# Reordered start of a two-layer attention, recurrence and mixture-of-experts kernel: inputs ahead of modulation weights, constants on another queue, a later softplus, idle matmuls

## Chip, cores and metric

The kernel runs on one core of one Trainium2 chip. The metric is the device time of one execution in microseconds (us), taken as the median of a few runs. One profiled execution, with its trace, is at hand as well. Engines are named as the profile names them: PE is the matrix engine, PEld its weight loads, DVE the vector engine, ACT the scalar engine, POOL the general engine, SP the engine that here issues nearly all transfers. A q behind a name (SPq, ACTq) is the engine's sequencer, which issues and waits.

## What is computed

Layer 0 modulates a normalised x and a normalised context with vectors that come out of the conditioning by a matrix product (`ada_w`), projects both, and runs attention over a neighbourhood and a gated linear recurrence side by side. Layer 1 mixes by a Fourier transform. Each layer ends with a mixture of 16 experts. The parts that the change touches:

```python
mod = silu_c @ ada_w[layer] + ada_b[layer]
shift1, scale1, gate1, shift2, scale2, gate2 = jnp.split(mod[:, None, :], 6, axis=-1)
h = modulate(rmsnorm(x, norm_mix[layer]), shift1, scale1)
...
h_ctx = modulate(rmsnorm(ctx, norm_mix[layer]), mod_ctx[:D], mod_ctx[D:])
...
log_a = -LRU_C * r * jax.nn.softplus(-lam.astype(jnp.float32))
return jnp.exp(log_a), jnp.sqrt(-jnp.expm1(2.0 * log_a)) * (i * xc)
```

x is 256 x 1024, the context 256 x 1024, everything in 32-bit floats.

## The kernel before

All weights pass through 16 slots of 1 MB. SP issues their transfers in the order of the program, and a slot's next transfer waits until the slot is given back. The order of instructions on each engine is set by a scheduler when the program is built; an engine then runs its list strictly in that order.

The first stage works in five units of one or two of the eight 128-channel blocks (`units0`). For a unit, `load_ada` (L268) brings the needed columns of four `ada_w` tiles in four pieces, `load_wx` (L272) brings rows of the first projection's weights. `ada_te` multiplies them with the conditioning on PE (L333, tile `gv`), ACT copies the result (L339, `gvr`), PE turns it into columns (L340), and DVE adds the bias (L350, `modc`, `modx`). Meanwhile `rms_scale` normalises x into `xn` and the context in place (`xc`): ACT squares and sums (L436) and takes the root (L438), DVE inverts and scales (L439, L440). PE transposes (L501, `tp`), ACT and DVE modulate (L513, L514, L516, giving the high part and the low part of h), `split_w` splits the weights into high and low parts (L394 on ACT, L395 on POOL or DVE, `wp`), and `channels` multiplies (L407 to L409, `xb`).

The next stage multiplies h with the key weights (`kp`), while DVE runs the convolution (L597, L600, `xcT`), further `ada_w` tiles in `ada_ve` (L375, L381, `gva`) and ACT the recurrence's gates: `Recurrence.gates` gives R and I by a sigmoid (L664), `Recurrence.scan` gives A by an exponential (L672, scale `spm8`) and a tanh (L673, scale `sp4`), then DVE `lt` (L679), ACT a root (L681), DVE L684 and further. `spm8` and `sp4` come from `softplus()` (L469 to L485), some 26 small DVE operations on 128x8 values in a row, which start from `softplus_exp()` (L462, L463 on ACT). The products `kp` are copied out by ACT and DVE (L619, L617, `kq`), and the query product (`qp`) takes over their PSUM banks.

A sigmoid, exponential, root or silu on ACT needs its table; where the table changes, the trace shows an ACT_TABLE_LOAD.

Of the kernel before, what the change touches and what calls it, by code (L numbers as in the profile page):

```python
# [12 lines left out]
AF = mybir.ActivationFunctionType  # L13
# [133 lines left out]
def hybrid_layers(  # L147
# [21 lines left out]
    nc = tc.nc  # L169
    ve, ac, te, gp = nc.vector, nc.scalar, nc.tensor, nc.gpsimd  # L170
# [8 lines left out]
    def acc(name="acc"):  # L179
        return ps.tile([128, 512], F32, tag="acc", name=name)  # L180
# [16 lines left out]
    def t2k(name):  # L197
        return buf(name, "t2k", 520, 4)
# [41 lines left out]
    smA = data.tile([94, 128], F32, tag="t1k", name="smA", bufs=2)  # L240
    smB = data.tile([96, 128], F32, tag="t1k", name="smB", bufs=2)
    cst = const.tile([128, 352], F32, name="cst")
    rw = const.tile([128, 8, 32], F32, name="rw")
    rb = const.tile([128, NE], F32, name="rb")
    nc.sync.dma_start(out=smA, in_=small[0:94, :])
    nc.sync.dma_start(out=smB, in_=small[94:190, :])
    nc.sync.dma_start(out=cst, in_=consts)
    ident = cst[:, 0:128]
    ones = cst[:, 128:256]
    iota1 = cst[:, 256:320]  # L250
# [11 lines left out]
    units0 = [(0,), (1,), (2, 3), (4, 5), (6, 7)]  # L262

    def load_ada(ks):
        c = slice(ks[0] % 4 * 128, ks[-1] % 4 * 128 + 128)
        for j in (ks[0] // 4, 2 + ks[0] // 4):
            for i in range(2):
                nc.sync.dma_start(out=a_s[j].part(i)[:, :, c], in_=a_s[j].src[i][:, :, c])  # L268
# [2 lines left out]
        i, k = divmod(k, 4)  # L271
        nc.sync.dma_start(out=Wx.part(i)[:, k:k + 2], in_=Wx.src[i][:, k:k + 2])  # L272

    load_ada(units0[0])
    for tb in range(2):
        nc.sync.dma_start(out=xt[:, tb], in_=x_in[tb * 128:(tb + 1) * 128, :])
    for tb in range(2):
        nc.sync.dma_start(out=xc[:, tb], in_=ctx_in[tb * 128:(tb + 1) * 128, :])
    load_wx(0)
# [20 lines left out]
    qn = cols[:, 92:93]  # L300
    kn = cols[:, 93:94]
    ada_b = [cols[:, 94:142], cols[:, 142:190]]

    sc32 = const.tile([128, 8, 32], F32, name="sc32")
    gp.memset(sc32, 0.0)
# [91 lines left out]
    def split_w(W, eng=gp):  # L397

        t = t4k("wp").bitcast(F32R)
        h, lo = t[:, 0:512], t[:, 512:1024]  # L400
        with tc.high_priority(PRI):
            split(h, W, lo, eng)
        return h, lo

    def mm3(p, lhs, rhs, start, stop):

        te.matmul(out=p, lhsT=lhs[0], rhs=rhs[0], start=start, stop=False)  # L407
        te.matmul(out=p, lhsT=lhs[0], rhs=rhs[1], start=False, stop=False)
        te.matmul(out=p, lhsT=lhs[1], rhs=rhs[0], start=False, stop=stop)  # L409

    def scale_col(name, mod, o, gain, s=slice(0, 8)):

        if name not in a_col:
            a_col[name] = const.tile([128, 8], F32, name=name)
        ve.scalar_tensor_tensor(a_col[name][:, s], mod[:, o + s.start:o + s.stop], 1.0, gain[:, s],
                                op0=ALU.add, op1=ALU.mult)
        return a_col[name]
# [43 lines left out]
    def softplus_exp():  # L461
        ac.activation(z, lam, AF.Abs)  # L462
        ac.activation(z, z, AF.Exp, scale=-1.0)  # L463
# [25 lines left out]
    hH = [h4[k // 4][:, k % 4] for k in range(8)]  # L489
# [7 lines left out]
    def transposed(k):  # L497
        p = wps("tp")
        for i in range(4):
            src = xn if i < 2 else xc  # L500
            te.transpose(p[:, i * 128:(i + 1) * 128], src[:, i % 2, k * 128:(k + 1) * 128], ident)  # L501
        return p

    def modulate(ps_):
        ks = sorted(ps_)
        s = slice(ks[0], ks[-1] + 1)
        a = scale_col("a1", modc[0], 8, g_mix[0], s)
        b = scale_col("a1x", modx, 8, g_mix[0], s)
        h = {}
        for k in ks:  # L510
            h[k] = t2k("hm")[:, 0:512]
            for c, m, sh in ((slice(0, 256), a, modc[0]), (slice(256, 512), b, modx)):
                ac.activation(hH[k][:, c], ps_[k][:, c], AF.Identity, scale=m[:, k:k + 1], bias=sh[:, k:k + 1])  # L513
                ve.tensor_scalar(h[k][:, c], ps_[k][:, c], m[:, k:k + 1], sh[:, k:k + 1], op0=ALU.mult, op1=ALU.add)  # L514
        for k in ks:
            ve.tensor_tensor(hL[k], h[k], hH[k].bitcast(F32), op=ALU.subtract)  # L516
# [7 lines left out]
    def channels(p, w, n, k):  # L524


        for b in range(4):
            c = slice(b * 128, (b + 1) * 128)
            first, last = (True, True) if n == 512 else (b % 2 == 0, b % 2 == 1)
            mm3(p[b], (w[0][:, c], w[1][:, c]), (hH[k][:, 0:n], hL[k][:, 0:n]), k == 0 and first, k == 7 and last)  # L530
# [4 lines left out]
    def ada_first(ks):  # L535
        ada_te(0, [(a_s[j], k % 4 * 128, 4 * j + k % 4) for j in (ks[0] // 4, 2 + ks[0] // 4) for k in ks], True)()

    wx = {}
    for u in range(len(units0) + 1):
        if u < len(units0):  # L540
            ks = units0[u]
            ada_first(ks)
            tp = {k: transposed(k) for k in ks}
            modulate(tp)
            for k in ks:
                wx[k] = split_w(Wx[:, k])
        if u == 1:
            softplus_exp()
        if u:
            for k in units0[u - 1]:  # L550
                channels(xp, wx.pop(k), 512, k)

    s_bg = [a_s[0].keep(i) for i in range(2)]
    s_kq = [a_s[2].keep(i) for i in range(2)]
# [322 lines left out]
    def normed(p4, gate, into=None):  # L877

        xn = t8k("xn").rearrange("p (t c) -> p t c", t=2) if into is None else into
        table(AF.Sqrt, p4[0][:, 0:1])  # L880
        for tb in range(2):
            for h in range(2):
                add_gated(p4[tb * 2 + h], gate, tb, slice(h * 512, (h + 1) * 512))
            last = rms_scale(xt, xn, tb)
        return xn, last
# [304 lines left out]
    xn, _ = normed(mp, gate)  # L1190
# [25 lines left out]
    for gp2 in range(2):  # L1216
# [5 lines left out]
        for b in range(2):  # L1222
            k = dict(start=(b == 0), stop=(b == 1))
# [21 lines left out]
    xn, _ = normed(mp, gate)  # L1245
# [81 lines left out]
```

## Time and profile before

| quantity | value |
|---|---|
| median of 3 runs | 803.24 us (802.31 to 805.01) |
| profiled execution, own time | 804.33 us |
| its span, first to last instruction | 802.5 us |
| PE busy | 712.6 us (89%) |
| DVE busy | 353.2 us (44%) |
| ACT busy | 236.9 us (30%) |
| POOL busy | 125.2 us (16%) |
| moved by DMA | 277.33 MB, mean 346 GB/s |

Busy shares are averages over stages with different limits. What the first stage is worth has to be read in its own stretch, and followed to the first place where another wait ends later.

### The profile page before, as it was taken

The numbers are of one execution on the slowest core, as the hardware profiler recorded it, in microseconds if no ns is written. First come the engines' busy times: TensorE is split into PE (matmuls) and PEld (weight loads), VectorE is DVE, ScalarE is ACT, GpSimd is POOL, SyncE is SP. The second block draws the span as 40 slices with busy tenths as digits, with TensorE's granted clock in tenths as the row PEclk, the third lists the DMA queues.
The fourth block names the chain that finished last, engine by engine and source line by source line (L and its number), as shares of the span: only waits on it lengthen the run. The fifth ranks groups of instructions, "written<-read, shape, count | busy, mean of one in ns | idle before, by whom it ended". The sixth has DMA issues, their size and how long they took to land. (4 is left out here: it accounts for less than half of the span.)

```text
span 802.5 us, 10368 instructions
## 1 busy us (share of the span) xinstructions
PE 712.6 (89%) x4080; PEld 388.7 (48%) x4080; DVE 353.2 (44%) x648; ACT 236.9 (30%) x420; POOL 125.2 (16%) x100
## 2 busy tenths in 40 slices
PE   3999869897998899799999996978699799999986
PEld 2676557674657534244344333656434344334333
DVE  3559798898875511111121105794421121112015
ACT  6246738554555310110111003434210110011000
POOL 1132561444111201000000001051201000000002
PEclk9999988897999899999999999999799999999999
DMA  8987467563887799999999999999199999999991
GB/s 278 360 331 294 169 262 263 212 261 125 342 325 287 291 354 421 418 414 422 419 423 420 420 421 421 421 409 367 60 423 421 401 423 421 421 423 419 422 376 63
DMA packets 53789, 277.33 MB, mean 346 GB/s; under 512 B 4898, under 2 KB 20832, under 8 KB 22496
## 3 DMA queue, kind: packets, MB, share of 16 engines
q1 hardware_dynamic: 53584, 276.47, 86.3%
q8 instruction: 36, 0.59, 0.3%
q14 instruction: 25, 0.20, 0.1%
q10 hardware_dynamic: 144, 0.07, 0.0%
HBM read 275.47 MB, written 1.05 MB: 345 GB/s over the span
## 5 line engine op out<-in xcount | busy, mean ns | idle before, releaser
L1054 PE MATMUL g<-slot,xg 128*64 128x512 f32 x512 | 116.2, 608 | 8.0 <-PEq L1142 8.0
L1091 PE MATMUL dn<-slot,aT 128*64 128x512 f32 (+1 forms) x544 | 115.7, 577 | 4.1 <-DVE aT L1075 4.1
L1054 PE MATMUL u<-slot,xg 128*64 128x512 f32 x512 | 113.7, 593 | 0.8 <-DMA slot<-in_moe_u_dram 0.8
L1060 DVE TENSOR_TENSOR act<-act,u 128x512 f32<-128x512 f32 x16 | 11.0, 687 | 191.2 <-PE u L1054 191.2
L395 POOL TENSOR_TENSOR wp<-slot,wp 128x512 fp32r<-128x512 f32 x41 | 60.3, 1480 | 155.9 <-ACT wp L394 145.9
L1054 PEld LDWEIGHTS g<-slot,xg 128*64 128x64 f32 x512 | 38.3, 140 | 82.0 <-issue 81.1
L1054 PEld LDWEIGHTS u<-slot,xg 128*64 128x64 f32 x512 | 38.8, 137 | 72.9 <-issue 70.9
L381 DVE SCALAR_TENSOR_TENSOR gva<-slot,sc,gva 128x512 f32<-128x512 f32 x77 | 72.6, 943 | 1.1
L1091 PEld LDWEIGHTS dn<-slot,aT 128*64 128x64 f32 x544 | 37.9, 138 | 70.6 <-issue 61.0
L1094 DVE SCALAR_TENSOR_TENSOR yL<-dn,gcol,yH 128x512 fp32r<-128x512 f32 (+1 forms) x34 | 24.5, 720 | 99.0 <-ACT yH L1093 90.8
L1093 ACT ACTIVATE yH<-dn,gcol 128x512 fp32r<-128x512 f32 (+1 forms) x34 | 22.5, 662 | 139.9 <-PE dn L1091 139.9
L1009 ACT ACTIVATE xg<-xg,modc,a 128x256 f32<-128x256 f32 x32 | 18.0, 564 | 136.4 <-PE xg L1000 136.4
L394 ACT ACTIVATE wp<-slot 128x512 fp32r<-128x512 f32 x72 | 43.8, 625 | 46.3 <-PE mix L409 15.8
L1011 POOL TENSOR_TENSOR SG<-S,gates 128x512 f32<-128x512 f32 x8 | 8.4, 1044 | 310.4 <-PE st L1063 302.0
L1059 ACT ACTIVATE act<-g 128x512 f32<-128x512 f32 x16 | 9.6, 597 | 121.0 <-PE g L1054 121.0
L333 PE MATMUL gv<-slot,sc 128*32 128x128 f32 x832 | 34.6, 297 | 6.5 <-DVE modc L350 3.7
L333 PEld LDWEIGHTS gv<-slot,sc 128*32 128x32 f32 x832 | 27.6, 119 | 13.3 <-DVE modc L350 3.9
L1000 PE MATMUL xg<-S,xh 128*128 128x256 f32 x128 | 28.4, 306 | 3.8 <-DVE S L988 2.6
L1007 DVE TENSOR_SCALAR xg<-xg,a,modc 128x256 f32<-128x256 f32 x32 | 17.4, 543 | 29.2 <-ACT xg L1009 29.2
L395 DVE TENSOR_TENSOR wp<-slot,wp 128x512 fp32r<-128x512 f32 x31 | 25.5, 826 | 8.0 <-ACT wp L394 7.3
L1000 PE MATMUL xg<-S,xl 128*128 128x256 f32 x128 | 27.4, 298 | 0.0
L1031 PE MATMUL ya<-yH,ST 128*128 128x512 f32 x60 | 26.4, 440 | 0.6 <-ACT yH L1093 0.2
(258 smaller groups left out, 1125.5 us busy)
## 6 DMA issues: line engine op xcount, KB each, us to landing
slot<-in_moe_g_dram SPq DMA_DIRECT2D x64, 1024.0 KB, 14.2
slot<-in_moe_u_dram SPq DMA_DIRECT2D x64, 1024.0 KB, 14.4
slot<-in_moe_d_dram SPq DMA_DIRECT2D x60, 1024.0 KB, 16.5
slot<-in_ada_w_dram SPq DMA_DIRECT2D x40, 1024.0 KB, 7.4
slot<-in_w_in_dram SPq DMA_DIRECT2D x8, 1024.0 KB, 8.3
slot<-in_ada_w_dram SPq DMA_DIRECT2D x12, 512.0 KB, 9.2
slot<-in_w_out_dram SPq DMA_DIRECT2D x4, 1024.0 KB, 4.9
slot<-in_fnet_w_dram SPq DMA_DIRECT2D x4, 1024.0 KB, 19.8
```

The costliest lines, as they stand in the source:

```text
L333: te.matmul(out=p[32 * q:32 * q + 32, 0:128], lhsT=sc32[:, k, :], rhs=W[:, k, c:c + 128], start=(k == 0), stop=(k == 7))
L381: ve.scalar_tensor_tensor(r, W[:, k], sc32[:, k, 0:1], r, op0=ALU.mult, op1=ALU.add)
L394: ac.activation(dst_h, src, AF.Copy)
L395: eng.tensor_tensor(dst_l, src, dst_h.bitcast(F32), op=ALU.subtract)
L1000: at_xg[0] = te.matmul(out=p[:, i * 256:(i + 1) * 256], lhsT=xx[:, tb, k * 128:(k + 1) * 128], rhs=S[:, tb * 256:(tb + 1) * 256], start=(n ...
L1007: ve.tensor_scalar(xg[:, k], pv, a2[:, k:k + 1], b2[:, k:k + 1], op0=ALU.mult, op1=ALU.add)
L1009: ac.activation(xg[:, k], pv, AF.Identity, scale=a2[:, k:k + 1], bias=b2[:, k:k + 1])
L1031: te.matmul(out=yacc[tb * 2 + h], lhsT=ST[:, tb * 128:(tb + 1) * 128], rhs=y[:, h * 512:(h + 1) * 512], start=(p == 0 and n == 0), stop=(n ...
L1054: te.matmul(out=q[half(i), :], lhsT=xg[:, k, half(i0 + i)], rhs=W[i][:, k], start=(k == 0), stop=(k == 7))
L1091: te.matmul(out=dn[half(i), :], lhsT=aT[:, fc * 128 + 64 * i:fc * 128 + 64 * i + 64], rhs=W[i][:, fc, c], start=(fc == 0), stop=(fc == 3))
L1093: ac.activation(yH[:, c], dn, AF.Copy, scale=gcol)
L1094: ve.scalar_tensor_tensor(yL[:, c], dn, gcol, yH[:, c].bitcast(F32), op0=ALU.mult, op1=ALU.subtract)
```

## The change

Four edits. The three small loads (`smA`, `smB`, `cst`) are issued by ACT in place of SP. The two loads of x are issued ahead of the first unit's four pieces of `ada_w`. Six matmuls on constants, into a PSUM tile that nobody reads, stand ahead of the first product with `ada_w`. `softplus_exp()` is tied behind the last modulating instruction of the first stage.

```diff
-    nc.sync.dma_start(out=smA, in_=small[0:94, :])
-    nc.sync.dma_start(out=smB, in_=small[94:190, :])
-    nc.sync.dma_start(out=cst, in_=consts)
+    nc.scalar.dma_start(out=smA, in_=small[0:94, :])
+    nc.scalar.dma_start(out=smB, in_=small[94:190, :])
+    nc.scalar.dma_start(out=cst, in_=consts)
...
-    load_ada(units0[0])
     for tb in range(2):
         nc.sync.dma_start(out=xt[:, tb], in_=x_in[tb * 128:(tb + 1) * 128, :])
+    load_ada(units0[0])
...
+    warm = acc("warm")
+    for _ in range(6):
+        te.matmul(out=warm[:, 0:352], lhsT=ones, rhs=cst, start=True, stop=True)
...
+    last_h = [None]
...
-                ac.activation(hH[k][:, c], ps_[k][:, c], AF.Identity, scale=m[:, k:k + 1], bias=sh[:, k:k + 1])
+                last_h[0] = ac.activation(hH[k][:, c], ps_[k][:, c], AF.Identity, scale=m[:, k:k + 1], bias=sh[:, k:k + 1])
...
-        if u == 1:
-            softplus_exp()
...
+    with tc.issue_after(last_h[0].ins):
+        softplus_exp()
```

The scheduler answers with another order on several engines; lines behind the edits have other numbers in the changed kernel (L436 becomes L441, L664 becomes L671, L672 becomes L679).

First place: ACT from the program's start. Before:

```order
L314 DMA before<-in_tri_dram 128x128
L306 ACT_TABLE_LOAD
L306 ACTIVATE sc_127<-cols 128x8x2
L462 ACTIVATE sp_145<-cols 128x8
L324 ACT_TABLE_LOAD
L324 ACTIVATE junk<-sc_127,eps 128x1
L463 ACT_TABLE_LOAD
L463 ACTIVATE sp_145<-sp_145 128x8
L436 ACTIVATE jk,ss<-xt 128x1024 x2
L438 ACT_TABLE_LOAD
L438 ACTIVATE rs<-ss,eps 128x1 x2
L436 ACTIVATE jk,ss<-xc 128x1024 x2
```

The same place in the changed kernel, from behind the three new issues on:

```order
L441 ACT_TABLE_LOAD
L441 ACTIVATE jk,ss<-xt 128x1024
L311 ACT_TABLE_LOAD
L311 ACTIVATE sc_134<-cols 128x8x2
L319 DMA before<-in_tri_dram 128x128
L329 ACT_TABLE_LOAD
L329 ACTIVATE junk<-sc_134,eps 128x1
L443 ACTIVATE rs<-ss,eps 128x1
L441 ACTIVATE jk,ss<-xt 128x1024
L344 ACTIVATE gvr<-gv 64x128
L443 ACTIVATE rs<-ss,eps 128x1
L441 ACTIVATE jk,ss<-xc 128x1024
```

The squares of x moved ahead of and around silu, one table load went, and the copy `gvr` of the first unit's product now stands ahead of the context's squares.

Second place: DVE in the key stage, where the tail of softplus now stands (`sp` are its small tiles; L485 to L490 are the old L480 to L485, L386 is `ada_ve`, L400 the split of a weight piece). In the changed kernel:

```order
L386 SCALAR_TENSOR_TENSOR gva<-slot_589,sc_134,gva 128x512
L485 TENSOR_TENSOR sp_762<-sp_762,sp_760 128x8
L486 TENSOR_SCALAR sp_762<-sp_762 128x8
L485 TENSOR_TENSOR sp_762<-sp_762,sp_760 128x8
L486 TENSOR_SCALAR sp_762<-sp_762 128x8
L487 TENSOR_TENSOR sp_762<-sp_762,sp_758 128x8
L488 SCALAR_TENSOR_TENSOR sp_762<-sp_762,sp_150 128x8
L489 TENSOR_SCALAR spm_154<-sp_762 128x8
L490 TENSOR_SCALAR sp4c<-sp_762 128x8
L400 TENSOR_TENSOR wp<-slot_595,wp 128x512
L394 TENSOR_TENSOR modc_147<-gv,cols 128x4
```

Before, softplus stood on DVE in the first stage, 22 of its operations ahead of the first L439 and the last four between the scalings of x. Now eight of its operations stand ahead of the convolution, eight more between `ada_ve` operations, and the last ten in a row just ahead of the first split of the query weights.

Third place: ACT in the key stage. Before:

```order
L664 ACT_TABLE_LOAD
L664 ACTIVATE R<-gp,cols 128x512
L672 ACT_TABLE_LOAD
L672 ACTIVATE A<-R,spm_147 128x512
L664 ACT_TABLE_LOAD
L664 ACTIVATE R<-gp,cols 128x512 x2
L394 ACTIVATE wp<-slot_120 128x512
L664 ACTIVATE R<-gp,cols 128x512
L673 ACTIVATE R<-R,sp4c 128x512
L394 ACTIVATE wp<-slot_588 128x512
L672 ACT_TABLE_LOAD
```

The same place in the changed kernel:

```order
L671 ACT_TABLE_LOAD
L671 ACTIVATE R<-gp,cols 128x512
L399 ACTIVATE wp<-slot_120 128x512
L671 ACTIVATE R<-gp,cols 128x512 x3
L679 ACT_TABLE_LOAD
L679 ACTIVATE A<-R,spm_154 128x512
L671 ACT_TABLE_LOAD
L671 ACTIVATE I<-gp,cols 128x512
L399 ACTIVATE wp<-slot_595 128x512
L671 ACTIVATE I<-gp,cols 128x512 x2
L680 ACTIVATE R<-R,sp4c 128x512
```

The first A (which reads `spm`) moved behind all four R. The four I, the first split of the query weights and the first tanh stand behind it. Over the whole program ACT has 22 table loads where it had 26. In the expert stages nothing moved.

## Rows read from the trace of the kernel before

**Rows 1.** The page's first line.

```profile
span 802.5 us, 10368 instructions
```

**Rows 2.** Busy time by stretch: stretch, its us, engines, granted clock, DMA share, GB/s.

```profile
30.00:35.00 5.00, 5.00 (x78) 3.91 (x78) 2.49 (x8) 1.32 (x3) 1.25 (x2) 1.00 1.08 364
```

**Rows 3.** Timeline of the first 27 us: start, us, engine, line, operation, idle before it.

```profile
0.74 0.37 SPq L245 DMA_DIRECT2D smA<-in_small_dram  x1
...
2.01 2.67 SPq L268 DMA_DIRECT2D slot<-in_ada_w_dram  x4
...
8.28 3.81 PE L333 MATMUL gv<-slot,sc 128*32 128x128 f32 x30 [0.79 <-DMA slot<-in_ada_w_dram]
...
10.18 1.46 PEld L333 LDWEIGHTS gv<-slot,sc 128*32 128x32 f32 x14 [0.44 <-DMA slot<-in_ada_w_dram]
...
11.39 1.06 ACT L436 ACTIVATE jk<-xt 128x1024 bf16<-128x1024 f32 x1 [1.37 <-DMA xt<-in_x_in_dram]
...
12.67 1.06 ACT L436 ACTIVATE jk<-xt 128x1024 bf16<-128x1024 f32 x1
...
20.21 1.57 DVE L440 TENSOR_SCALAR xc<-xc,rs 128x1024 f32<-128x1024 f32 x1
...
22.35 0.56 ACT L513 ACTIVATE h<-tp,modc,a 128x256 fp32r<-128x256 f32 x1 [3.09 <-PE tp L501]
22.67 3.63 PE L333 MATMUL gv<-slot,sc 128*32 128x128 f32 x32
...
26.23 1.13 PE L407 MATMUL xb<-h,wp 128*128 128x512 f32 x2
```

**Rows 4.** One piece for the fourth unit: its issue, its landing; the unit's first product.

```profile
L268 SPq DMA_DIRECT2D slot<-in_ada_w_dram x1: 1461/1461/1461, 23.7 to 23.7; - x1
...
DMA to landing us min/median/max: 9.7/9.7/9.7
...
35.87 0.41 PE L333 MATMUL gv<-slot,sc 128*32 128x128 f32 x4
```

**Rows 5.** Timeline, DVE: the first and last of 18 alternating softplus operations.

```profile
10.91 0.17 DVE L480 TENSOR_TENSOR sp<-sp,sp 128x8 f32<-128x8 f32 x1
...
14.37 0.17 DVE L481 TENSOR_SCALAR sp<-sp 128x8 f32<-128x8 f32 x1
```

**Rows 6.** Timeline from the first to the second stage: ACT, DVE and PE.

```profile
59.05 0.63 ACT L394 ACTIVATE wp<-slot 128x512 fp32r<-128x512 f32 x1 [2.76 <-PE xb L409]
...
74.14 0.72 ACT L672 ACTIVATE A<-R,spm 128x512 f32<-128x512 f32 x1
...
80.55 1.28 ACT L672 ACT_TABLE_LOAD   x1
...
81.00 0.68 DVE L395 TENSOR_TENSOR wp<-slot,wp 128x512 fp32r<-128x512 f32 x1
...
86.41 0.16 DVE L389 TENSOR_TENSOR modc<-gv,cols 128x4 f32<-128x4 f32 x1 [4.74 <-PE gv L386]
...
87.48 5.08 DVE L381 SCALAR_TENSOR_TENSOR gva<-slot,sc,gva 128x512 f32<-128x512 f32 x3
...
96.42 0.69 DVE L617 COPY kq<-kp 128x512 f32<-128x512 f32 x1
...
97.16 0.51 PE L407 MATMUL qp<-wp,h 128*128 128x512 f32 x1 [3.29 <-DVE kq L617]
...
98.17 0.63 ACT L394 ACTIVATE wp<-slot 128x512 fp32r<-128x512 f32 x1 [3.33 <-PE qp L409]
...
100.78 1.09 DVE L684 SCALAR_TENSOR_TENSOR A<-A,R 128x512 f32<-128x512 f32 x1 [0.61 <-ACT R L681]
```

**Rows 7.** Timeline, second direction of the recurrence: ACT and DVE.

```profile
157.14 0.63 ACT L394 ACTIVATE wp<-slot 128x512 fp32r<-128x512 f32 x1 [6.97 <-PE vp L409]
...
158.42 1.28 DVE L679 SCALAR_TENSOR_TENSOR lt<-A,R 128x512 f32<-128x512 f32 x1 [2.12 <-ACT R L673]
```

**Rows 8.** Busy time by stretch, as in the second group, after two waits of PE.

```profile
110.00:120.00 10.00, 4.17 (x17) 3.58 (x17) 10.00 (x11) 1.43 (x3) 6.07 (x5) 0.79 0.56 227
```

## The prediction

> **What bounds the kernel now.** I read the share of each stretch first, then the timeline of the first 27 us, then the waits from the key product on. The span is 802.5 us of a profiled execution of 804.33 us, so 1.8 us lie outside it [rows 1]. From 22.67 us PE works without a gap worth naming [rows 2, 3], and it stays so for some 70 us. Ahead of that it waits. The reader should follow one chain: x lands at 11.39 us and its second half lets ACT go on at 12.67, ACT then squares and takes roots of x and of the context, DVE scales the context's second half at 20.21 (1.57 us), the four transposes follow, and the first modulated block starts on ACT at 22.35 us [rows 3]. Only then come 32 products for the second unit (3.63 us), and the first projection product stands at 26.23. The product for the first unit with `ada_w` was long ready: its last 14 records could start at 10.18, when the last piece landed, and ended at 8.28 + 3.81 = 12.1 us [rows 3]. So x is late and `ada_w` is early, and the DMA engines are full from then on (share 1.08 [rows 2]): what one gains the other gives.
>
> From the key product on, another chain decides: the key product's banks are copied out by DVE at 96.42, PE waits 3.29 us for that, ACT then waits 3.33 us for PE, and DVE goes on with the recurrence at 100.78 [rows 6].
>
> **Part 1, the head: x first, constants from ACT.** SP loses three issues, which held it from 0.74 until the first piece at 2.01: the large transfers start 1.27 us sooner [rows 3]. The set of constants, four pieces and x was in at 12.67 (the square started as soon as it could). With 1.27 us won, the same set is in at about 11.4, with the pieces now last. Bounds for the last piece: 10.18 (as now) and 12.67 (it simply takes x's place). I take 11.4.
>
> Then, in the new order on ACT: the second half of the product takes 1.9 us (10.18 to 12.1 [rows 3]), to 13.3; the copy and root 0.5, to 13.8; the context's first square with its read 1.25 (11.39 to 12.67 is one square and the start of the next, 1.28 [rows 3]), a root 0.2, the second square 1.25, a root 0.2: 16.7; DVE scales, between half of 1.57 and 1.57 us, and PE transposes 0.5: about 18.4. Against 22.35 that is 4.0 us. With the bounds of the last piece it is 5.2 and 2.7. Softplus leaving DVE gives nothing here, since DVE had been waiting for ACT's roots.
>
> Does the gain last to the key product? The second unit's products and everything behind them come 4.0 earlier, and the pieces of later units must be there. For the fourth unit the last piece lands at 23.7 + 9.7 = 33.4, the one that its first product needs about 1.5 us before (estimate: the issue of the last took 1461 ns, the queue being full), and the product starts at 35.87 [rows 4]. That leaves 4.0, and 1.27 more by the earlier stream: enough, but a gain over 5 would end there. So: -4.0.
>
> A rule of the skill speaks against this edit, and I weigh it here. The Trainium skill, DMA: Bandwidth & Descriptors, section "Issuing engines are not separate DMA queues", says that transfers issued from several engines run on the same 16 DMA engines, so that only issue time is saved. The trace bears on it by the share of 1.08 [rows 2]: a full set of engines has nothing to give. The sum above uses the 1.27 us of issue alone; what an exchange without that would give is a rival below.
>
> **Part 2, the idle matmuls.** Six calls of 352 columns are twelve records. Two records of 512 columns took 1.13 us at 26.23 [rows 3], so twelve of 352 take at most 12 x 0.565 x 352/512 = 4.7 us. They start when the constants are in, and PE now waits until 8.28 for a piece [rows 3], which will land later than now. Cost 0, covered by that wait; were the constants in so late that they end at 10, up to 1 us. On the good side: 32 records of 128 columns in 3.63 us at 22.67 are 113 ns each, which is the lower of the clock's two levels (128 columns at 1.2 GHz are 107 ns). Were the last half of the first unit's product at the higher level, it would take 0.95 us less. PE waits for pieces in between, so I count 0 of it, and keep -0.95 as a bound.
>
> **Part 3, softplus moved.** ACT's exponential and its table load (1.28 us [rows 6]) fall into a wait of 2.76 us for PE at 59.05 [rows 6]: no cost. The 26 DVE operations are the matter. Alternating in a row they step by (14.37 - 10.91)/17 = 0.204 us [rows 5]. Eight stand ahead of the convolution (1.6 us, of which 1.1 fall into DVE's wait for the same ACT piece), eight are spread between longer operations and cost some 0.3. The last ten stand in front of the split at 81.00 [rows 6]: ten by 0.204 is 2.0. All times here are on the old trace's clock; the head's gain shifts them together. From 81.0, less 0.6 for the `lt` that no longer stands there, plus 0.8, plus 2.0, `spm8` is there at about 83.1. DVE itself loses nothing, since it now waits 4.74 us until 86.41 [rows 6].
>
> But ACT used `spm8` at 74.14 [rows 6]. In the new order its first A waits for 83.1, and behind it, in strict order: load 1.28, A 0.72, load 1.28, one I 0.7, the first split of the query weights 0.63, two I 1.3, tanh 0.7: 89.7. Less, in the bargain, are two of six table loads up to here. DVE's `lt` needs that tanh, and now stands ahead of the `ada_ve` run that begins at 87.48 [rows 6]. So DVE is 2.2 us late, and its copy of the key product comes at 98.6 in place of 96.42. PE's wait grows from 3.29 to 5.5, ACT's split at 98.17 comes at 100.4. Between that split and the first root there stand now one more tanh and one more split, 0.7 + 0.6: DVE's L684 comes at 100.78 + 2.2 + 1.3 = 104.3, 3.5 late. Of that 0.2 to 0.6 lie in its present wait of 0.61 [rows 6]; I take 3.3. Bounds: 1.2, if DVE's run gets shorter by being later (the three operations at 87.48 take 1.7 us each, the four behind them, until 96.42, only 1.0 each, so 2.1 could be had); 5.5, if PE runs at the lower level after its longer wait (below). From there DVE has no slack for 20 us, so it stays: +3.3.
>
> On the price of a table load page and trace differ: the Trainium skill, ScalarE: Activation LUTs, section "What ACT_TABLE_LOAD costs", gives about 2.66 us for every switch, load and drain together. The row shows 1.28 and the next operation right behind [rows 6]; by the page's figure the wait above would be 2.8 us longer for its two loads (an estimate), and the measurement decides.
>
> **Part 4, further down.** In the recurrence's second direction two more loads go. ACT's split at 157.14, which waited 6.97 us for PE, still stands ahead of the second tanh, and DVE's 2.12 us wait at 158.42 with it [rows 7]. 0; bounds -1.5 and +1.
>
> **Sum.** -4.0 + 0 + 3.3 + 0 = -0.7: 803.6 for the profiled execution's own 804.33. That execution is 1.09 above the median of 803.24, so the median goes to about 802.5.
>
> **Rivals.** *The loss fades*: the head's 4.0 reaches the end, since DVE's lateness is taken up by waits it has anyway (4.74 at 86.41, 2.12 at 158.42 [rows 6, 7]) and by two saved loads at the second place. For it: many waits between engines there; against it: DVE is the last one in the chain at 96.42 and 100.78. -4.0 + 0.4 = -3.6: 799.6.
>
> *Slower*: PE's wait of 5.5 us for the key product's copy brings its clock down. After waits at 110 to 120 us the granted clock is 0.79 of full on average, so part of it at the lower level [rows 8]. The query product is 48 products of some 0.23 us; half of them at half speed cost 5.6 us, of which PE's later slack takes a part. -4.0 + 3.3 + 4.0 = +3.3: 806.5. It decides where the granted clock in the 10 us behind that copy is under about 0.8.
>
> *An exchange, no more*: x and the pieces swap places, the last piece lands at 12.67, the head gives 2.7. -2.7 + 3.3 = +0.6: 803.8. By the rule on issuing engines above this is what to expect if issue time was not what held the stream.
>
> **Numbers.** Forecast (-0.7) 0.37, fading loss 0.34, slower by clock 0.19, exchange 0.10. No change within 0.3% (2.4 us), about what a measurement here can tell. The forecast's own range is 800.3 (5.2 in the head, 2.2 lost) to 805.6. Same: 0.33 of the forecast and the exchange, 0.43; faster 0.36; slower 0.21. The range of 8 in 10 reaches from 797.8 (the fading loss with 5.2 in the head and something saved) to 806.5.
>
> **What would show it.** The first L520 at 18.4 (right) or past 20 (exchange); the last piece of the first unit at about 11.4; first A on ACT behind an idle time of some 5 us that `spm` ends; PE's wait for `kq` at 5 us or more; the granted clock behind it. I am wrong if ACT does not wait for `spm`, or if what is lost there is made up before 230 us.

## The result, and the profile after

The changed kernel takes 808.48 us in the median of 6 executions (806.08 to 810.09), the kernel before 802.87 beside it: a ratio of 1.0065, 95% interval 1.0045 to 1.0084. It is slower by 5.6 us, outside the range of the prediction. The profiled execution took 807.81 us:

```profile
span 806.0 us, 10378 instructions
```

The head of the changed kernel, from its timeline (start, us, engine, line, operation, idle before it and what ended that):

```profile
0.74 0.87 SPq L275 DMA_DIRECT2D xt<-in_x_in_dram  x2
1.66 4.64 SPq L268 DMA_DIRECT2D slot<-in_ada_w_dram  x4
1.66 0.44 ACTq L247 DMA_DIRECT2D cst<-in_consts_dram  x1
7.80 0.39 PE L290 MATMUL w<-cst,smA 94*128 94x94 f32 x1 [7.80 <-DMA cst<-in_consts_dram]
8.14 6.36 PE L307 MATMUL warm<-cst 128*128 128x352 f32 x12
14.43 1.94 PE L338 MATMUL gv<-slot,sc 128*32 128x128 f32 x32
16.42 0.27 ACT L344 ACTIVATE gvr<-gv 64x128 f32<-64x128 f32 x1 [3.25 <-PE gv L338]
16.78 1.04 ACT L441 ACTIVATE jk<-xc 128x1024 bf16<-128x1024 f32 x1
21.16 0.56 ACT L520 ACTIVATE h<-tp,modc,a 128x256 fp32r<-128x256 f32 x1 [0.52 <-PE tp L506]
22.24 3.62 PE L338 MATMUL gv<-slot,sc 128*32 128x128 f32 x30
25.79 0.80 PE L412 MATMUL xb<-h,wp 128*128 128x512 f32 x1
```

Read against [rows 3]: the large transfers do leave earlier, at 0.74 and 1.66 us instead of 2.01. But the constants, issued at 1.66 by ACT, are waited for until 7.80. Twelve idle records then hold PE for 6.36 us. The first unit's product, which stood at 8.28, starts at 14.43, and ACT, which has to copy it (`gvr`) before it squares the context, waits 3.25 us for it. The first modulated block comes at 21.16 instead of 22.35, not at 18.4 as forecast, and the second unit's product still takes 3.62 us: the granted clock is 1.00 from 13.5 to 20 us, while PE works off the first unit's product in 1.94 us, and 0.50 from 20.5 to 27 us. The first projection product is 0.44 us earlier than before (25.79 instead of 26.23), and that is lost again soon: at 37.91 PE waits 0.97 us for ACT's modulated h, where no wait of PE between 26 and 60 us was longer than 0.3 us before.

```profile
37.91 0.97 PE L412 MATMUL xb<-h,wp 128*128 128x512 f32 x3 [0.97 <-ACT h L520]
```

The key stage, from the same timeline (DVE, ACT, PE):

```profile
83.72 0.16 DVE L490 TENSOR_SCALAR sp4c<-sp 128x8 f32<-128x8 f32 x1
83.89 1.28 ACT L679 ACT_TABLE_LOAD   x1 [5.39 <-DVE sp4c L490]
85.19 0.72 ACT L679 ACTIVATE A<-R,spm 128x512 f32<-128x512 f32 x1
88.46 1.35 DVE L400 TENSOR_TENSOR wp<-slot,wp 128x512 fp32r<-128x512 f32 x1 [4.58 <-ACT wp L399]
100.29 0.68 DVE L624 COPY kq<-kp 128x512 f32<-128x512 f32 x1
101.03 0.79 PE L412 MATMUL qp<-wp,h 128*128 128x512 f32 x1 [5.07 <-DVE kq L624]
102.71 0.63 ACT L399 ACTIVATE wp<-slot 128x512 fp32r<-128x512 f32 x1 [4.93 <-PE qp L414]
105.33 0.63 ACT L399 ACTIVATE wp<-slot 128x512 fp32r<-128x512 f32 x1 [1.38 <-PE qp L414]
107.94 0.69 DVE L691 SCALAR_TENSOR_TENSOR A<-A,R 128x512 f32<-128x512 f32 x1 [2.22 <-ACT R L688]
```

Nearly all of this chain is the forecast one. ACT waits 5.39 us for DVE's tail of softplus. DVE then waits 4.58 us for ACT's split, which stands behind that wait, two table loads, A and an I (I had expected it to wait for the tanh behind them); DVE is late with the copy of the key product (100.29, [rows 6] had 96.42); PE waits 5.07 us for it in place of 3.29; and the recurrence goes on at 107.94 in place of 100.78. Busy time by stretch (us of the stretch, PE, PEld, DVE, ACT, POOL, granted clock, DMA share, GB/s):

```profile
30.00:35.00 5.00, 5.00 (x78) 3.58 (x75) 1.16 (x7) 1.10 (x3) 0.23 (x1) 1.00 1.08 364
97.00:105.00 8.00, 3.97 (x9) 3.14 (x10) 7.89 (x11) 2.02 (x4) 2.05 (x2) 0.61 0.52 161
```

PE is full from 30 to 35 us as in [rows 2]. From 97 to 105 it is busy for half of the time, at a mean granted clock of 0.61, so mostly at the lower of the two levels.

### The profile page after: what moved, and what is told of

Its sections match the earlier page's. It is cut to its first block, busy times and chain, and to the rows that moved or that the text cites. A ratio compares the mean times of both kernels' runs of the same rounds, so it can differ in the third digit from the quotient of the medians.

```text
span 806.0 us, 10378 instructions
## 1 busy us (share of the span) xinstructions
PE 715.1 (89%) x4092; PEld 388.0 (48%) x4092; DVE 352.7 (44%) x648; ACT 231.7 (29%) x416; POOL 127.1 (16%) x100
## 5 line engine op out<-in xcount | busy, mean ns | idle before, releaser
L400 POOL TENSOR_TENSOR wp<-slot,wp 128x512 fp32r<-128x512 f32 x41 | 59.8, 1468 | 153.3 <-ACT wp L399 153.3
L386 DVE SCALAR_TENSOR_TENSOR gva<-slot,sc,gva 128x512 f32<-128x512 f32 x77 | 70.1, 911 | 1.0
L338 PE MATMUL gv<-slot,sc 128*32 128x128 f32 x832 | 32.9, 291 | 4.6 <-DVE modc L355 4.6
L400 DVE TENSOR_TENSOR wp<-slot,wp 128x512 fp32r<-128x512 f32 x31 | 26.0, 847 | 11.7 <-ACT wp L399 10.9
## 6 DMA issues: line engine op xcount, KB each, us to landing
slot<-in_moe_g_dram SPq DMA_DIRECT2D x64, 1024.0 KB, 13.5
```

The source lines that it names most:

```text
L338: te.matmul(out=p[32 * q:32 * q + 32, 0:128], lhsT=sc32[:, k, :], rhs=W[:, k, c:c + 128], start=(k == 0), stop=(k == 7))
L386: ve.scalar_tensor_tensor(r, W[:, k], sc32[:, k, 0:1], r, op0=ALU.mult, op1=ALU.add)
L400: eng.tensor_tensor(dst_l, src, dst_h.bitcast(F32), op=ALU.subtract)
```

## Experiments

Theory: two losses. The idle matmuls behind late constants take the head's gain, and the wait for `spm` costs more than the 3.3 us that I gave it. Rivals: one of the two alone; the lower clock; the order of A and R on ACT. To keep head and key stage apart I read two numbers from each trace: **A** is the start of PE's instructions less the start of the same ones in the kernel before, as the median over those that began between 50 and 60 us there; **B** is the same for DVE between 110 and 120 us. In between lies the key stage, so B - A is what it costs. Each run is an edit together with the order that the scheduler answers with, so a difference between two runs is the price of both.

**One edit undone, or one alone.** `late` stands for softplus' exponential behind the first stage.

```diff
# u3: the changed kernel
-    with tc.issue_after(last_h[0].ins):
-        softplus_exp()
+        if u == 1:
+            softplus_exp()
# u4: the changed kernel
-    warm = acc("warm")
-    for _ in range(6):
-        te.matmul(out=warm[:, 0:352], lhsT=ones, rhs=cst, start=True, stop=True)
# u1: the changed kernel, smA, smB and cst alike
-    nc.scalar.dma_start(out=cst, in_=consts)
+    nc.sync.dma_start(out=cst, in_=consts)
# o3: the kernel before, last_h as in the change
-        if u == 1:
-            softplus_exp()
+    with tc.issue_after(last_h[0].ins):
+        softplus_exp()
```

> The changed kernel with softplus' exponential where it was before (behind the second unit); the other three edits stay. Theory (the moved softplus carries the loss: ACT's first A waits 5.4 us for spm, PE 5.1 us for kq, and PE's granted clock falls to 0.5 from 98.7 to 105.6 us): ACT's A stands near 75 us again with no wait for spm, PE's wait for kq is back at about 3.3 us, the clock there stays at 1.0, and of the 5.6 us only the head's 1.0 us is left: 803.4 to 804.5. Rival (the head carries it: idle matmuls, late constants, and what PE's early activity does to its clock later): 806.5 or more, with the half clock near 100 us still there.

> The changed kernel without the six idle matmuls; the rest stays. In the trace of the changed kernel they hold PE from 8.14 to 14.50 us, and the first unit's product starts only then. Theory (softplus carries the loss, the idle matmuls take about 2 to 3 us of the head): the product starts at about 11.5 us in the cold and takes 3.6 us, the copy gvr stands at about 15.3 instead of 16.4, the head comes 1 us earlier, so by 90 us PE is level with the kernel before (+1.0 gone), and the time is 806.5 to 807.5. Rival (the idle matmuls carry the whole loss): 803.0. Rival (they pay by the clock): 809 or more.

> The changed kernel with the three small loads issued by SP ahead of x again; x still stands ahead of the first pieces of ada_w, idle matmuls and softplus stay as changed. In the changed kernel smB and cst land at 7.16 and 7.67 us behind x, before at 3.79 and 4.13. Theory (they came late because they share the DMA engines with x): they land at about 4 us, silu stands at 6.6, the idle matmuls end at about 11.2 instead of 14.5, the first unit's product at about 12.5 to 13.5; the first modulating instruction at 19 to 20 instead of 21.2, so 1 to 2 us less than the changed kernel: 806.5 to 807.5, the rest being softplus. Rival (the queue of the small loads is worth nothing, x decides): within 0.5 us of the changed kernel. Rival (the queue carries the whole loss): 803.

> The kernel before with softplus' exponential moved behind the first stage, and nothing else. Theory (softplus carries the loss): ACT's first A waits some 5 us for spm, PE 5 us for kq, the granted clock falls behind that, and the time is 806.5 to 808.5, the whole loss without the other edits. My prediction's step priced it at 3.3, which would be 806.2. Rival (the loss fades by the end, as in the second case of the prediction): 803.3. Rival (the head carries the loss): 802.5 to 803.5, though A waits.

Measured: u3 804.64 us (ratio 1.0010, 0.9995 to 1.0026), u4 807.26 (1.0054, 1.0038 to 1.0070), u1 805.64 (1.0032, 1.0016 to 1.0047), o3 806.00 (1.0031, 1.0019 to 1.0044). With softplus early the wait for `spm` is gone, PE waits 3.33 us for `kq` again, and B - A falls from 5.0 to -0.1: the key stage's loss is softplus'. In o3, which has no other edit, the whole chain stands again; it is 3.0 us slower than the kernel before, where I had expected 3.5 to 5.5. Its timeline (DVE, POOL, ACT, PE):

```profile
16.52 0.75 DVE L440 TENSOR_SCALAR xc<-xc,rs 128x1024 f32<-128x1024 f32 x1
17.89 0.75 DVE L440 TENSOR_SCALAR xc<-xc,rs 128x1024 f32<-128x1024 f32 x1
18.25 2.73 POOL L395 TENSOR_TENSOR wp<-slot,wp 128x512 fp32r<-128x512 f32 x2 [8.45 <-ACT wp L394]
19.21 0.56 ACT L515 ACTIVATE h<-tp,modc,a 128x256 fp32r<-128x256 f32 x1 [0.51 <-PE tp L501]
80.69 1.28 ACT L674 ACT_TABLE_LOAD   x1 [5.40 <-DVE sp4c L485]
97.84 0.79 PE L407 MATMUL qp<-wp,h 128*128 128x512 f32 x1 [5.07 <-DVE kq L619]
```

I had not expected the first four rows: softplus' move alone brings the first modulated block from 22.35 to 19.21. ACT's roots now follow their squares with no table load and no weight split between, so DVE scales the context before POOL subtracts on `wp`, in 0.75 us each (1.57 in [rows 3]). By A it is 2.1 us: 1.0 us goes on a wait of PE for h at 34.72, as at 37.91 in the changed kernel.

In u4 the product comes 3.9 us earlier, though it takes 3.63 us, and the first modulated block at 18.93, near the forecast's 18.4:

```profile
10.51 3.63 PE L335 MATMUL gv<-slot,sc 128*32 128x128 f32 x32 [2.04 <-ACT sc L308]
14.18 0.27 ACT L341 ACTIVATE gvr<-gv 64x128 f32<-64x128 f32 x1 [0.90 <-PE gv L335]
18.93 0.56 ACT L517 ACTIVATE h<-tp,modc,a 128x256 fp32r<-128x256 f32 x1 [0.52 <-PE tp L503]
```

So the six matmuls cost the head 3.3 us (A from +1.1 to -2.2), more than the 1 us that I had expected of their removal; 2.2 of it stand at the first modulated block already. In u1 the same six are harmless, since they start when the constants land on SP's queue; the product behind them takes 1.94 instead of 3.6 us, and the run, expected at 806.5 to 807.5, is faster than that:

```profile
4.31 0.39 PE L290 MATMUL w<-cst,smA 94*128 94x94 f32 x1 [4.31 <-DMA cst<-in_consts_dram]
4.65 6.05 PE L307 MATMUL warm<-cst 128*128 128x352 f32 x12
11.82 1.94 PE L338 MATMUL gv<-slot,sc 128*32 128x128 f32 x30 [0.79 <-DMA slot<-in_ada_w_dram]
```

**x first, and softplus in two other places.** o2 is the kernel before with x first; c has x first and `late`. In b4 the exponential stands behind the first unit; in b1 it stands as in the change, but its DVE operations are called for at once (`tail`).

```diff
# o2, c: the kernel before (c with late)
-    load_ada(units0[0])
     for tb in range(2):
         nc.sync.dma_start(out=xt[:, tb], in_=x_in[tb * 128:(tb + 1) * 128, :])
+    load_ada(units0[0])
# b4: the kernel before, last_h as in the change
         if u == 1:
-            softplus_exp()
+            with tc.issue_after(last_h[0].ins):
+                softplus_exp()
# b1: the kernel before, with late (tail)
     with tc.issue_after(last_h[0].ins):
         softplus_exp()
+    softplus()
...
-        if n == 4:
-            softplus()
```

> The kernel before with x issued ahead of the first unit's pieces of ada_w, and nothing else. Prediction's step: x early is worth about 2.7 us of the head by itself (4.0 with the issue time saved), so PE stands 2.7 us earlier at 30 us, and the time is about 800.3. Theory now: it is an exchange. With the small loads on SP, x lands at 7.6 and 8.9 us (seen in the run with the constants on SP) and the pieces one after the other up to 12.6; the last half of the first unit's product waits for that, ACT's copy gvr stands behind it, and DVE still scales the context beside POOL's split of wp, at 1.5 us each: -0.5 to +0.5 at 30 us, 802.5 to 803.5.

> x first and softplus late, constants on SP, no idle matmuls: the changed kernel without two of its edits. With softplus alone PE stands at -2.3 us from 30 to 90 us and at +2.0 behind 100 us (run of softplus alone); with constants on SP but the idle matmuls kept at -2.6 and +2.0. Theory (x first is an exchange, and idle matmuls cost nothing once the constants are there at 4 us, since PE waits for pieces until 11.8 anyway): -2.3 to -2.8 at 30 us, +2 behind 100 us, 805 to 806. Rival (idle matmuls cost even then): -4 at 30 us, 804. Rival (they pay by the clock, the first unit's product taking 3.6 instead of 1.9 us): -1 at 30 us, 806.5.

> The kernel before with softplus' exponential tied behind the first unit's last modulating instruction, so between the old place (ahead of x's square) and the changed one (behind the whole first stage). Softplus alone, moved all the way, took 2.2 us off the head (ACT's roots stand behind their squares, so DVE scales the context ahead of POOL's split of wp, 0.75 us each instead of 1.5) and gave 4.3 back near 100 us. Theory (the two are separate: the head gains by what no longer stands there, the loss comes from spm alone being late): -2.2 at 40 us is kept, spm is ready before ACT's first A, PE's wait for kq stays near 3.3, and the time is 800 to 801.5. Rival (the later loss comes from the other order of A and R on ACT, not from the wait for spm): the loss of about 4 stays, 804.5 to 806. Rival (some 26 small DVE operations inside the first stage cost what they save): 803.

> The kernel before with softplus' exponential behind the first stage as in the change, but its DVE operations called for at once, so that they stand among the convolution's and not ahead of the first split of the query weights. Theory (the wait for spm is the loss): spm is ready at about 65 to 70 us, ACT's first A no longer waits 5 us for it, PE's wait for kq is back at some 3 to 4 us, the head's -2.2 stays to the end: 800 to 802. Rival (DVE's ten operations weigh where they stand, whatever waits for them): the convolution and the later ada_ve run end 4 to 5 us later, 803 to 804. Rival (order of A and R on ACT): 804.5 to 806.

Measured: o2 806.51 (1.0051, 1.0021 to 1.0081), c 808.55 (1.0064, 1.0042 to 1.0085), b4 803.38 (1.0000, 0.9990 to 1.0010), b1 803.23 (1.0003, 0.9982 to 1.0024). x first is not even an exchange: by A it costs 2.4 us alone and 2.1 with `late` (c against o3). Here my second theory missed as well, for both runs. o2's timeline (PE, ACT, POOL, DVE):

```profile
12.34 3.62 PE L333 MATMUL gv<-slot,sc 128*32 128x128 f32 x30 [0.92 <-DMA slot<-in_ada_w_dram]
16.00 0.27 ACT L339 ACTIVATE gvr<-gv 64x128 f32<-64x128 f32 x1 [0.45 <-PE gv L333]
16.29 1.28 ACT L438 ACT_TABLE_LOAD   x1
17.78 1.04 ACT L436 ACTIVATE jk<-xc 128x1024 bf16<-128x1024 f32 x1
19.51 2.94 POOL L395 TENSOR_TENSOR wp<-slot,wp 128x512 fp32r<-128x512 f32 x2 [8.70 <-ACT wp L394]
19.55 1.77 DVE L440 TENSOR_SCALAR xc<-xc,rs 128x1024 f32<-128x1024 f32 x1
23.61 0.75 DVE L440 TENSOR_SCALAR xc<-xc,rs 128x1024 f32<-128x1024 f32 x1
24.93 0.57 ACT L513 ACTIVATE h<-tp,modc,a 128x256 fp32r<-128x256 f32 x1 [4.79 <-PE tp L501]
```

The pieces land last, the product ends at 16.0 instead of 12.1, and its copy stands on ACT ahead of the context's second square at 17.78, with a table load between them. In the kernel before that square stood ahead of the copy, at 16.56:

```profile
16.56 1.04 ACT L436 ACTIVATE jk<-xc 128x1024 bf16<-128x1024 f32 x1
```

The product had slack while x was late, and x first takes that slack away. But this is not all of o2's loss, and the parts are not separated: softplus' operations now stand on DVE between the two scalings of the context, so the second one comes at 23.61 instead of 20.21, though its root on ACT began at 19.34. In c softplus is gone from there and the context's second square is even 0.3 us earlier than in o3 (15.87, 16.20). There the second scaling meets POOL's subtraction:

```profile
17.92 1.82 DVE L442 TENSOR_SCALAR xc<-xc,rs 128x1024 f32<-128x1024 f32 x1
```

That is 1.1 us longer than in o3, and the second unit's product takes 3.62 us instead of 2.92. u1 has the pair the other way round: its idle matmuls end in time and shorten the first unit's product, the second scaling comes ahead of POOL, and A is 2.6 us better than in c.

In b1 ACT's wait for `spm` is down to 1.69 us, PE waits 3.33 us for `kq`, and B - A is 1.0. But the scheduler also gave b1 the kernel before's order of A and R:

```profile
72.48 1.28 ACT L675 ACT_TABLE_LOAD   x1 [1.69 <-DVE sp4c L485]
73.78 0.72 ACT L675 ACTIVATE A<-R,spm 128x512 f32<-128x512 f32 x1
76.33 1.85 ACT L667 ACTIVATE R<-gp,cols 128x512 f32<-128x512 f32 x3
```

So no run has the late `spm` without the order R, R, R, R, A, or the other way round, and the rival by the order is not ruled out. The trace shows that both take part: the late `spm` sets when ACT goes on, and the order puts the loads, A and I ahead of the split that DVE waits 4.58 us for. The median of b1, 803.23, is above the 800 to 802 that I had expected. b4 has 2.4 us at 30 us and loses them by 50, where PE waits 2.37 us for ACT's h, with softplus' operations now inside the first stage.

**All four edits with one size or place changed, and two combinations.** i2 has two idle matmuls, a1 the changed kernel with `tail`, b3 x first, six idle matmuls and `late` with `tail` (constants on SP), o4 idle matmuls alone.

```diff
# i2: the changed kernel
-    for _ in range(6):
+    for _ in range(2):
# a1: the changed kernel with tail; b3: a1 with the constants on nc.sync
# o4: the kernel before
+    warm = acc("warm")
+    for _ in range(6):
+        te.matmul(out=warm[:, 0:352], lhsT=ones, rhs=cst, start=True, stop=True)
```

> The changed kernel, all four edits kept, with softplus' DVE operations called for right behind its exponential, so that spm is ready before ACT's first A. Theory (the wait of 5.4 us for spm is the whole of what is lost near 100 us): PE stands at +1.0 from 30 to 90 us as in the changed kernel, PE's wait for kq is 3.3 us instead of 5.1, at 100 to 130 us PE and DVE stand at +1.5 to +2.5 instead of +5 to +6, and the time is 804 to 806, some 3 to 4 under the changed kernel. Rival (a lower clock behind PE's start near 20 us or another order is the cause): +5 stays, 808.

> The changed kernel with two idle matmuls instead of six (four records, about 2.1 us by 0.53 us each, from 8.1 to 10.2 us). Theory (the six cost 3.4 us of the head because, with the constants in at 7.7 us, they end at 14.5 us, behind the last piece of ada_w at about 11.5): the two end before the last piece lands, so they cost at most 0.2, and PE stands at -2 to -3 from 30 to 90 us, as without any; then about +2 behind 100 us: 805 to 807. Rival (any idle matmul costs, by the other order or the lower clock at 20 us): +1 stays at 30 us, 808.

> The changed kernel without the two things that the runs blame: constants on SP as before, and softplus' DVE operations early; x first, idle matmuls and the later exponential stay. From the run with constants on SP (PE at -2.6 from 30 to 90 us) and the one with the tail early (spm no longer waited for, 1 us given back by 80 us): -2.7 at 40 us, about -1.5 from 100 us on, 801 to 802. Rival (what is won in the head is given back somewhere whatever stands in it): 803 to 804.

> The kernel before with the six idle matmuls alone. The constants are there at 4.1 us, so they run from 4.7 to about 10.7; the last piece of ada_w lands at 10.1. The first unit's product then runs at the higher level and ends at about 12.6 instead of 12.1; nothing waits for it, since ACT copies it at 19.0. Theory (Part 2's zero was right for constants that land early): 0 to +0.5 in the head, 802.5 to 803.5. Rival (they keep the clock up and the second unit's product, 3.63 us before, gets shorter): -1 to -2 at 30 us, 801.5. Rival (they cost even so): +1, 804.

Measured: a1 804.44 (1.0030, 1.0001 to 1.0058), i2 805.19 (1.0013, 0.9995 to 1.0030), b3 802.12 (1.0005, 0.9980 to 1.0030), o4 803.35 (0.9988, 0.9973 to 1.0004). The first three came about as expected. In o4 the second unit's product takes 2.96 us instead of 3.63 and A is -1.3, but the median does not show it. Two idle matmuls end in time; the product behind them takes 2.67 us, in between:

```profile
7.97 2.61 PE L307 MATMUL warm<-cst 128*128 128x352 f32 x4
10.51 2.67 PE L338 MATMUL gv<-slot,sc 128*32 128x128 f32 x32
```

**The last three.** d2 is all four edits with two idle matmuls and `tail`; o1 the kernel before with the constants on ACT's queue and nothing else; d1 the kernel before with six idle matmuls, `late` and `tail`.

```diff
# o1: the kernel before, smA, smB and cst alike
-    nc.sync.dma_start(out=cst, in_=consts)
+    nc.scalar.dma_start(out=cst, in_=consts)
# d2: i2 and a1 together; d1: o4 and b1 together
```

> All four edits of the change, with two idle matmuls instead of six and softplus' DVE operations called for right behind its exponential. Theory (the two causes are the whole loss): PE at -3.4 from 30 to 60 us as with two idle matmuls, -2.4 from 80 us on, no wait for spm, PE's wait for kq 3.3 us; -2.4 from 100 to 150 us, 800.5 to 802. Rival (something else in the edits costs, further down): level with the kernel before or above it, 803 to 806.

> The kernel before with the three small loads issued by ACT, and nothing else. Prediction's step: SP's first piece goes out 1.27 us sooner, so all large transfers land 1.3 us sooner, x's second half at about 11.4 instead of 12.65, and the constants as early as before: -1.0 to -1.3 at 30 us. Theory now: the large ones do land 1 to 1.3 us sooner, but the constants 2.5 to 3.5 us later, behind the pieces, at about 6.5 to 7.5; silu stands near 9.5, the first unit's product starts near 9.8 in place of 6.9 and ends at about 13.4, which nothing waits for, since ACT copies it at 19; softplus' chain on ACT, load and exponential, now stands between silu and the square of x and holds that up: 0 to +1.5 at 30 us, 803 to 804.5. Rival (an exchange without gain: the engines are full, so nothing lands sooner): x at 12.6, 803 to 804.

> The kernel before with the six idle matmuls, the later exponential and softplus' DVE operations early; constants and x as before. From the runs: softplus late gives -2.2 in the head and, with its tail early, -0.8 from 80 us on; idle matmuls alone -1.3 from 30 us on. Theory (both are kept, as they shorten different waits): -3 at 40 us, -2 at 100 us, 800.5 to 802, the fastest of all. Rival (they shorten the same wait, the second unit's product): -2.2 at 40 us, -0.8 at 100, 802.5.

Measured: d2 801.28 (0.9991, 0.9969 to 1.0012), o1 800.67 (0.9972, 0.9957 to 0.9986), d1 803.30 (1.0014, 0.9988 to 1.0040). o1 beats both the kernel before, by 2.6 us, and the changed one, and it is the only run whose interval lies wholly under 1; I had expected no gain. Its timeline (PE, ACT):

```profile
6.73 0.39 PE L290 MATMUL w<-cst,smA 94*128 94x94 f32 x1 [6.73 <-DMA cst<-in_consts_dram]
9.32 3.62 PE L333 MATMUL gv<-slot,sc 128*32 128x128 f32 x32 [2.04 <-ACT sc L306]
11.91 1.04 ACT L436 ACTIVATE jk<-xt 128x1024 bf16<-128x1024 f32 x1
```

The constants are 2.4 us later than on SP's queue here too (4.31 in u1), and the product with them, but nothing waits for it yet; x's second square starts at 11.91 instead of 12.67. That 0.8 us is not how the run gains, though. The first modulated block comes at 24.46, 2.1 us later than before, and the first projection product at 26.54, 0.3 later. What is earlier is the second unit's product, which PE now works off ahead of the context's last transposes, from 21.05 instead of 22.67:

```profile
21.05 3.11 PE L333 MATMUL gv<-slot,sc 128*32 128x128 f32 x30
24.46 0.56 ACT L513 ACTIVATE h<-tp,modc,a 128x256 fp32r<-128x256 f32 x1
```

d1 was to be the fastest of all, at 800.5 to 802; the head gave 2.4 us and not 3, and the median is level.

All runs beside each other, A, B and B - A in us, worked out as said above:

```
run      const. x first idle softplus   A     B    B-A   median
changed  ACT    yes     6    late      +1.1  +6.1  5.0   808.48
u4       ACT    yes     0    late      -2.2  +2.5  4.7   807.26
i2       ACT    yes     2    late      -3.3  +1.7  5.0   805.19
u1       SP     yes     6    late      -2.6  +2.5  5.1   805.64
c        SP     yes     0    late       0.0  +5.1  5.1   808.55
o3       SP     no      0    late      -2.1  +2.5  4.6   806.00
a1       ACT    yes     6    tail       0.0  +1.5  1.5   804.44
d2       ACT    yes     2    tail      -3.5  -2.0  1.5   801.28
b3       SP     yes     6    tail      -2.6  -1.7  0.9   802.12
b1       SP     no      0    tail      -1.8  -0.8  1.0   803.23
d1       SP     no      6    tail      -2.4  -1.4  1.0   803.30
u3       ACT    yes     6    early     +1.7  +1.6 -0.1   804.64
o2       SP     yes     0    early     +2.4  +2.4  0.0   806.51
o4       SP     no      6    early     -1.3  -1.2  0.1   803.35
o1       ACT    no      0    early     -2.4  -2.4  0.0   800.67
b4       SP     no      0    unit 1    +0.3  +0.3  0.0   803.38
```

The median less that of the kernel before follows B within 1.5 us, but for u4 (1.8). So what is lost or won by 110 us reaches the end.

## Why the prediction was wrong

**The step that failed is Part 2's "Cost 0, covered by that wait"**, on two counts. Its cover was a wait that begins when the constants are in, and I took them to be in as early as before; behind x on the same DMA engines they came 3.5 us later. And the size was scaled from a product on fp32r inputs, 4.7 us at most, where records with f32 inputs took 6.36 (5.40 to 6.52 over the runs with six). The scaling by columns left out the weight load of 0.34 us that stands in front of each record; these loads follow each other by 0.59 us here. How much of the difference that makes was not tried:

```profile
8.79 0.34 PEld L307 LDWEIGHTS warm<-cst 128*128 128x128 f32 x1 [0.25 <-issue]
9.37 0.34 PEld L307 LDWEIGHTS warm<-cst 128*128 128x128 f32 x1 [0.25 <-issue]
```

The bound of 1 us for "end at 10" shows that I saw the mechanism and not its reach: they ended at 14.5. u4 and i2 show the price: 3.3 us against none, 4.4 against two. This is the largest of the three misses; Part 1 missed by 1.8 (-4.0 forecast, -2.2 in u4) and Part 3 by 1.7.

**Part 1's sum of -4.0 had the wrong parts.** Taken one by one, the queue brings 2.4 (o1; 2.2 as u4 against c), x first costs 2.4 (o2; 2.1), and softplus' leaving, which I had put at nothing, brings 2.1 (o3; 2.4 as c against o2): -2.1 together, and u4, which has these three, stands at -2.2. The forecast of the first modulated block was good without the idle matmuls (18.93 in u4, 18.4 forecast). What failed there is the step "Does the gain last to the key product?": I asked it of the landing of later pieces alone, and 1.0 us went on PE's wait for ACT's h in a later unit.

That the queue's gain is the 1.27 us of issue time is not shown. In o1 it comes with another order on PE. In u4 the second scaling of the context starts at 17.60, 0.3 us earlier than in c, and so 0.4 us ahead of POOL's subtraction; it takes 0.76 us instead of 1.82, which alone is about half of the 2.2. x alone was not what held the head: the first unit's product is nearly as late, and takes over when x is moved ahead of its pieces. So the rival *exchange* was too kind to that edit.

The rule weighed in Part 1 (the Trainium skill, DMA: Bandwidth & Descriptors, "Issuing engines are not separate DMA queues") agrees with the trace in kind: the large transfers left up to 1.27 us earlier, and the constants, which had to share the engines with x, were usable at 7.80 instead of 4.27. By that rule I should have asked where the constants would land.

**Part 3's mechanism, the late `spm` in the new order, was right, its size too small.** The wait for `spm`, PE's wait of 5.07 (5.5 forecast) and the late recurrence are in the trace. The term was 3.3; B - A is 4.6 to 5.1 in all six runs with `late`, inside the bounds of 1.2 to 5.5. In the changed kernel a part of the difference is the row at 105.33: a second split on ACT, which I had at 0.6 us, waits another 1.38 us for PE's query products. Another is DVE's copy, 3.9 us late, of which 0.9 come from the head: 3.0 instead of the 2.2 forecast.

**The rival by the clock** named its sign, a granted clock under 0.8 behind the copy, and the sign came: 0.61. It does not carry the loss. From 97 to 107 us the mean clock is 0.66 in a1, where B - A is 1.5, and 0.83 in o3, where it is 4.6. It is 0.83 in u3 and o2 too, where B - A is -0.1 and 0.0. Some 0.5 us can be the clock's at most, by what the changed kernel has more than o3 (an estimate from these two). The rows are a1's and o3's:

```profile
97.00:107.00 10.00, 8.91 (x27) 7.08 (x28) 6.96 (x12) 5.40 (x9) 4.58 (x3) 0.66 0.59 227
```

```profile
97.00:107.00 10.00, 9.16 (x38) 7.54 (x39) 8.28 (x11) 6.39 (x10) 4.76 (x3) 0.83 0.72 285
```

**Together:** +1.1 in the head instead of -4.0, and 5.0 instead of 3.3 in the key stage, are +6.1 at 110 us; the median gave 5.6. Part 4's zero for what lies further down holds in so far. The loss is not made up before 230 us, as the rival of the fading loss would have it: PE stands at +6.1 from 200 to 250 us. In this one pair of traces 2.5 us of it are gone by 500 us, in c's none. One sum of the prediction does not come out: its own bounds, 2.7 in the head and 5.5 lost, give 806.0 as the upper end of the forecast's range and not 805.6. d2, with all four edits and these two causes taken away, is level with the kernel before or slightly below it, so no third cause of that size is left.

**Open:** behind 150 us the executions spread more than the edits explain. a1 has 12 between 800.5 and 811.7 us, four of them above 811, and its profiled one is among those; b1, b3, d1 and o2 have two or three each that stand some 5 to 9 us above the middle of their others. In a1's trace the differences of start grow from +1.5 us at 150 us to +8 at 350. In a1, b3, d1 and o2 these executions have the lowest mean granted clocks of their kernel (0.943 in all four of a1's, 0.951 to 0.958 in its others). Whether the clock makes the time or follows from it was not tried. Open too is how the key stage's loss divides between the late `spm` and the order on ACT.

## What to carry to other kernels

Filler work hidden in a wait is only as safe as the event that starts it: price it from rows of the same input type, and ask whether the same change delays that event. Before moving one of two inputs ahead, find out how much slack the other has, and what stands behind it in a strictly ordered queue. A long chain of tiny operations costs little where it stands and much where its result is awaited; calling for it at once gave back 3.5 of 5.0 us (a1, d2), together with the order that the scheduler then chose. A gain of a few tenths of a microsecond can decide which of two engines comes first, and so be worth 1 us (u4 against c) or nothing: ask of a small edit what else it reorders.

## What the runs showed of the hardware

Small loads on a second queue did not pass the large ones on the first: 176 KB issued at about 1.7 us were usable at 7.80 behind x, at 6.73 behind the `ada_w` pieces, and at 4.3 when issued ahead on one queue.

DVE's scaling of 128x1024 took 0.75 us alone and 1.77 where POOL's subtraction had started just before it (19.51 and 19.55 in o2). The Trainium skill, SBUF — State Buffer, section "Who interferes with whom", says that a tensor_scalar on DVE can run in a mode in which it and an operation on GpSimd (POOL here) exclude each other, and that the one that issues second is blocked meanwhile. The rows agree in kind: the 1.0 us more is less than one of POOL's two operations (2.94 us for both).

The first unit's product took 3.6 us after an idle PE, 2.67 behind four idle records and 1.94 behind twelve, at the cost of 2.61 and, by run, 5.4 to 6.5 us of PE.
